# Attention in a macaron encoder layer: where the splits of the projection weights may run, and how the fourth part's projection steps are spread

## The chip, the cores and the metric

The kernel runs on one core of a Trainium2 chip. The metric is the device time in microseconds. The profile names five engines: PE (TensorE: matrix products and transposes; PEld is its weight load), DVE (VectorE), ACT (ScalarE), POOL (GpSimd) and SP (SyncE, which issues the DMAs).

## The reference

One layer: x = x + ½ SwiGLU(norm(x)), then x = x + attention(norm(x)), then x = x + ½ SwiGLU(norm(x)), for 1024 rows of 1024 in float32. The change lies in the attention, a stick-breaking one with 16 heads of 64:

```python
qkv = (xn @ w_qkv).reshape(b, s, 3, SB_HEADS, SB_HEAD_DIM)
q = rms_norm(qkv[:, :, 0], q_gain).astype(jnp.float32).transpose(0, 2, 1, 3)
k = rms_norm(qkv[:, :, 1], k_gain).astype(jnp.float32).transpose(0, 2, 1, 3)
v = qkv[:, :, 2].astype(jnp.float32).transpose(0, 2, 1, 3)
...
    z = jnp.einsum('bhqd,bhkd->bhqk', q[:, :, lo:hi], k[:, :, :hi]) * scale
...
    log_beta = jax.nn.log_sigmoid(z)
    log_1m = jnp.where(mask, jax.nn.log_sigmoid(-z), 0.0)
    rev = lax.cumsum(log_1m, axis=3, reverse=True)
...
    w = jnp.where(mask, jnp.exp(log_beta + rev_excl), 0.0)
    outs.append(jnp.einsum('bhqk,bhkd->bhqd', w, v[:, :, :hi]))
```

## The kernel before

Every product is made of three: an operand is split into a rounded high part (ScalarE copies it into the format that TensorE multiplies) and a low part (raw minus high), and TensorE computes high·high, high·low and low·high (lines 255 to 257). So weights must be split before they are used.

The attention works on heads in **pairs**, 0 to 7. Its plan is a list of (nominal time, step): `PAIR` is 61, cut into the parts a (10), b (14), c (21) and d (16). For every pair `put` and `spread` enter the steps at such times; sorted by them, they are traced. The time is only an order: the tile framework then gives each engine its queue, taking what was traced first where several instructions are ready, and bringing forward later ones whose inputs and buffers are there. Within an engine's queue the order is then fixed.

In the turn of pair p stand:

- **scores** (lines 750 to 785) of four units, head 0 or 1 and half 1 or 0 of the queries. TensorE multiplies (L770), ScalarE takes two sigmoids (L774), VectorE scans (L776), GpSimd sets the first column (L781) and multiplies (L783). The unit of part d belongs already to pair p+1.
- **values** (lines 787 to 842) of the unit scored one part before: TensorE transposes w (L805), ScalarE and VectorE split it into th and tl (L168, L169), TensorE multiplies by v (L823). A finished half goes out through SyncE (L837).
- the **projection of pair p+1**, `qkv`: 24 steps, that is two halves of the rows (half 1 first), four blocks of 128 rows in each, three *thirds* of the eight 128-deep slices of the weights in each block (slices 0 to 2, 3 to 5, 6 and 7). `FILLS` says how many of them lie in each part: 4, 6, 8, 6. After the last third of a block `finish` squares and copies (L692, L693, ScalarE), and after the fourth block of a half VectorE works out the norms (L180 to L184), then r (L704), and GpSimd doubles the keys (L708 for head 0, L711 for head 1). The fourth block of half 1 ends early in c; the third block of half 0 is the first three steps of d, its fourth the last three.
- **prep_q** and **prep_k**: TensorE transposes queries and keys (L728), ScalarE and VectorE split them (L732, L733). `prep_k(nxt, 0, 1)` stands at c 17.5, `prep_q(this, 0)` at a 5.0 and `prep_k(this, 0, 0)` at a 7.5; the last two read half 0, which ended in d of the turn before, and prep_k what L708 wrote.
- the **weights of pair p+2**, `weights_of`, in pairs 0 to 5: four steps of two slices each. A step loads 2 x 192 KB into one of two buffers `raw_qkv` (L657, two DMAs of SyncE), ScalarE makes the high part (L660) and GpSimd two low parts (L663). Slices 0 to 3 and 4 to 7 have a tile each for high and low; four such sets take turns (`wq0` to `wq3`), so those of pair p+2 are written where those of pair p stood. `LOADS` puts the steps at a 6.0, b 8.0, d 2.0 and d 8.0. They need nothing but their raw data and the set of tiles, which the projection of pair p frees at the end of the turn p-1.

The last turn in which weights are split is that of pair 5; the turn of pair 6 still projects pair 7, that of pair 7 projects nothing.

Of the kernel before, what the change touches and what calls it, by code (L numbers as in the profile page):

```python
# [13 lines left out]
ALU = mybir.AluOpType  # L14
# [28 lines left out]

FILLS = {"a": 4, "b": 6, "c": 8, "d": 6}

LOADS = (("a", 6.0), ("b", 8.0), ("d", 2.0), ("d", 8.0))

SHARES = (("b", 6.0), ("b", 11.0), ("c", 3.0), ("c", 9.0), ("c", 15.0), ("d", 1.5), ("d", 5.0), ("d", 8.5))

# [49 lines left out]
def macaron_kernel(ctx, tc, x, g1, w1_in, w1_out, gm, w_qkv, gq, gk, w_o, g2, w2_in, w2_out, out):  # L99
    nc = tc.nc  # L100
    act, dve, pool_e, pe, sp = nc.scalar, nc.vector, nc.gpsimd, nc.tensor, nc.sync
# [533 lines left out]
    with ExitStack() as stack:  # L635
# [6 lines left out]
            sp.dma_start(t, src)  # L642
            g_sb.append(t)

        def weights_of(p, state):

            wh, wl = state["wq"] = {}, {}

            def step(k):
                if k % 4 == 0:  # L650
                    wq = pl[f"wq{(2 * p + k // 4) % 4}"]
                    state["h"], state["l"] = (wq.tile([P, 4, 3 * P], F32R, name=f"wq{n}", bufs=1) for n in "hl")
                h_, l_ = state["h"], state["l"]
                raw = pl["raw_qkv"].tile([P, 2, 3, P], F32, name="raw_qkv")
                src = w_qkv[k * P : (k + 2) * P, :].rearrange("(k p) (a c) -> p k a c", p=P, a=3)
                for i in range(2):
                    sp.dma_start(raw[:, i], src[:, i, :, p * P : (p + 1) * P])  # L657
                ks = slice(k % 4, k % 4 + 2)
                raw = raw.rearrange("p k a c -> p k (a c)")
                act.activation(h_[:, ks], raw, AF.Copy)  # L660
                for i in range(2):
                    k_ = k % 4 + i
                    pool_e.tensor_tensor(l_[:, k_, :], raw[:, i, :], h_[:, k_, :].bitcast(F32), op=ALU.subtract)  # L663
                    wh[k + i], wl[k + i] = h_[:, k % 4 + i, :], l_[:, k % 4 + i, :]

            return [partial(step, k) for k in ((4, 6, 0, 2) if p == 0 else (0, 2, 4, 6))]

        def qkv(p, state):

# [181 lines left out]
        states = [{} for _ in range(NP)]  # L851
        plan = []

        def spread(steps, t0, t1, at=0.5):
            plan.extend((t0 + (t1 - t0) * (i + at) / len(steps), f) for i, f in enumerate(steps))

        steps = qkv(0, states[0])
        for f in weights_of(0, states[0]):
            f()
# [8 lines left out]
        dve.tensor_copy(first[:, :P], ident)  # L868
        spread(steps[12:], -26.0, -6.0)
        spread(weights_of(1, states[1]), -20.0, -2.0)  # L870
        for p in range(-1, NP):
            this = states[p] if p >= 0 else None
            nxt = states[p + 1] if p < NP - 1 else None
            start, t = {}, PAIR * p
            for part, span in PARTS.items():
                start[part], t = t, t + span

            def put(part, t, f):
                plan.append((start[part] + t, f))

            for part, span in PARTS.items():
                state = nxt if part == "d" else this
                if state is not None:
                    spread(scores(state, *UNITS[part]), start[part], start[part] + span, 0.5)
                if this is not None:
                    groups = values(this, p, *BEFORE[part])
                    for i, (to_turn, to_apply) in enumerate(groups):
                        t = TURN + (span - TURN) * i / len(groups)
                        put(part, t, to_turn)
                        put(part, t + APPLY, to_apply)  # L890
            if nxt is not None:
                if p >= 0:
                    fills = qkv(p + 1, nxt)
                    for part, span in PARTS.items():
                        for i in range(FILLS[part]):
                            put(part, span * (i + 0.5) / FILLS[part], fills.pop(0))
                put("c", 15.0, partial(prep_q, nxt, 1))
                put("c", 17.5, partial(prep_k, nxt, 0, 1))
                put("d", 8.0, partial(prep_k, nxt, 1, 1))
            if this is not None:  # L900
                put("a", 5.0, partial(prep_q, this, 0))
                put("a", 7.5, partial(prep_k, this, 0, 0))
                put("b", 8.0, partial(prep_k, this, 1, 0))
            if 0 <= p < NP - 2:
                for at, f in zip(LOADS, weights_of(p + 2, states[p + 2])):
                    put(*at, f)
            if p == NP - 2:
                put("c", 10.0, partial(load_o, 1))
                put("d", 15.5, lambda: marks.append(tc.cur_priority))
            if p == NP - 1:  # L910
                put("a", 2.5, partial(load_o, 0))
                for at in SHARES:
                    put(*at, lambda: marks.append(tc.cur_priority))
# [126 lines left out]
```

## Time and profile before

| | us |
|---|---|
| median of 3 runs | 1998.88 (1997.27 to 1999.94) |
| the profiled execution | 1997.53 |
| its span | 1995.8 |
| of it: first feed-forward and norm, 0 to 657 | 657.0, TensorE busy 632.7 |
| first projections, 657 to 743 | 86.0, TensorE busy 76.4 |
| pairs, 743 to 1230 | 487.0, TensorE busy 464.6 |
| output projection and second feed-forward | 765.8, TensorE busy 752.4 |

The stretches come from the table of windows. In lists in order of time a row has start, duration, engine, line and operation, what it writes and reads, how many were merged, and in brackets the idle time of the engine before it and what ended that. The list of waits has the waiter, the one that ended the wait, the sum in us, how often, and the longest. A window's row has the length, then busy time and count of PE, PEld, DVE, ACT and POOL, the share of its clock that TensorE was granted, the share of time of the DMA engines, and GB/s. Where a window is asked for one line alone, only that line's engine stands in it.

### The profile page before, as it was taken

The numbers are of one execution on the slowest core, as the hardware profiler recorded it, in microseconds if no ns is written. First come the engines' busy times: TensorE is split into PE (matmuls) and PEld (weight loads), VectorE is DVE, ScalarE is ACT, GpSimd is POOL, SyncE is SP. The second block draws the span as 40 slices with busy tenths as digits, with TensorE's granted clock in tenths as the row PEclk, the third lists the DMA queues.
The fourth block names the chain that finished last, engine by engine and source line by source line (L and its number), as shares of the span: only waits on it lengthen the run. The fifth ranks groups of instructions, "written<-read, shape, count | busy, mean of one in ns | idle before, by whom it ended". The sixth has DMA issues, their size and how long they took to land.

```text
span 1995.8 us, 27301 instructions
## 1 busy us (share of the span) xinstructions
PE 1926.1 (97%) x9656; PEld 1651.9 (83%) x9656; DVE 1252.9 (63%) x1793; ACT 988.1 (50%) x1802; POOL 1092.0 (55%) x921
## 2 busy tenths in 40 slices
PE   7899999999999999999999999999999999999999
PEld 6788888887888789888888997779888888888887
DVE  6945644645675957768777787566654554547644
ACT  6443343343334557777777777443444334344332
POOL 2666666755456634655555455113666666755454
PEclk9999999999999999999999999999999999999999
DMA  5132332337997410111011045222332323359884
GB/s 206 64 101 101 116 101 85 126 113 261 332 320 256 139 39 13 54 43 38 28 54 38 14 145 169 85 90 64 122 101 90 122 96 101 105 190 359 317 270 152
DMA packets 168505, 260.26 MB, mean 130 GB/s; under 512 B 11568, under 2 KB 81200, under 8 KB 168368
## 3 DMA queue, kind: packets, MB, share of 16 engines
q1 hardware_dynamic: 168368, 258.52, 38.1%
q8 instruction: 75, 1.23, 0.2%
q14 instruction: 62, 0.51, 0.1%
HBM read 198.18 MB, written 60.29 MB: 130 GB/s over the span
## 4 chain that ended last, share of the span: by engine, by line
PE 79%; DVE 9%; POOL 4%; ACT 4%; issue 2%; DMA 1%; SPq 0%; ACTq 0%; POOLq 0%; DVEq 0%
PE ka L255 6%; PE ka L256 6%; PE ka L257 6%; PE kc L257 4%; PE kc L256 4%; PE kc L255 4%; PE bq L256 4%; PE bq L255 4%; PE bq L257 4%; PE ma L255 4%; PE kb L255 4%; PE kb L257 3%; PE kb L256 3%; PE ma L257 3%; PE ma L256 3%; PE bo L823 3%
## 5 line engine op out<-in xcount | busy, mean ns | idle before, releaser
L169 POOL TENSOR_TENSOR u<-sf,u 128x512 fp32r<-128x512 f32 x160 | 226.6, 1418 | 161.2 <-ACT u L168 160.4
L169 POOL TENSOR_TENSOR rp<-raw,rp 128x1024 fp32r<-128x1024 f32 x84 | 208.7, 2487 | 185.1 <-ACT rp L168 172.9
L169 POOL TENSOR_TENSOR u<-raw,u 128x512 fp32r<-128x512 f32 x136 | 199.8, 1473 | 167.3 <-ACT u L168 167.2
L783 POOL TENSOR_TENSOR w<-w,om 128x512 f32<-128x512 f32 (+4 forms) x128 | 140.8, 1103 | 142.1 <-DVE om L776 115.4
L168 ACT ACTIVATE u<-sf 128x512 fp32r<-128x512 f32 x160 | 100.9, 631 | 217.7 <-PE kb L256 89.8
L363 DVE TENSOR_TENSOR h<-h 128x512 f32<-128x512 f32 x110 | 134.7, 1228 | 90.0 <-POOL h L464 89.3
L255 PE MATMUL bq<-wqh,xh 128*128 128x384 f32 x512 | 177.7, 347 | 2.8 <-DVE vst L697 2.8
L168 ACT ACTIVATE rp<-rh 128x1024 fp32r<-128x1024 f32 (+1 forms) x78 | 76.6, 984 | 207.0 <-issue 86.5
L257 PE MATMUL bq<-wqh,xl 128*128 128x384 f32 x512 | 174.4, 341 | 0.0
L256 PE MATMUL bq<-wql,xh 128*128 128x384 f32 x512 | 174.3, 341 | 0.0
L255 PE MATMUL ka<-xh,u 128*128 128x512 f32 (+1 forms) x448 | 163.2, 365 | 9.8 <-ACT s L413 7.6
L256 PE MATMUL ka<-xl,u 128*128 128x512 f32 (+1 forms) x448 | 163.0, 364 | 1.2 <-DVE xl L169 1.2
L257 PE MATMUL ka<-xh,u 128*128 128x512 f32 (+1 forms) x448 | 162.6, 363 | 0.0
L168 ACT ACTIVATE u<-raw 128x512 fp32r<-128x512 f32 x136 | 84.6, 631 | 148.4 <-PE ka L256 101.8
L485 DVE TENSOR_TENSOR raw<-raw 128x1024 f32<-128x1024 f32 (+1 forms) x60 | 85.2, 1421 | 108.7 <-DMA raw<-w_out 97.6
L255 PE MATMUL ma<-rp 128*128 128x512 f32 x352 | 137.9, 392 | 2.0 <-DVE h L417 2.0
L774 ACT ACTIVATE w<-bz,f 128x512 f32<-128x512 f32 (+1 forms) x192 | 112.2, 584 | 55.5 <-PE bz L770 54.3
L256 PE MATMUL ma<-rp 128*128 128x512 f32 x352 | 137.6, 391 | 0.0
L257 PE MATMUL ma<-rp 128*128 128x512 f32 x352 | 137.5, 390 | 0.0
L390 DVE TENSOR_TENSOR sf<-raw 128x512 f32<-128x512 f32 x80 | 79.1, 990 | 89.3 <-POOL u L169 89.3
L464 POOL TENSOR_TENSOR h<-h,g 128x512 f32<-128x512 f32 x80 | 112.1, 1401 | 29.0 <-DVE h L417 29.0
L169 DVE TENSOR_TENSOR tl<-bt,th 128x512 fp32r<-128x512 f32 (+1 forms) x160 | 105.0, 657 | 30.1 <-ACT th L168 28.3
(219 smaller groups left out, 5573.7 us busy)
## 6 DMA issues: line engine op xcount, KB each, us to landing
raw<-w_out SPq DMA_DIRECT2D x120, 512.0 KB, 5.4
raw<-w_in SPq DMA_DIRECT2D x88, 512.0 KB, 3.6
k<-h SPq DMA_DIRECT2D x154, 256.0 KB, 2.0
rh<-k SPq DMA_DIRECT2D x64, 512.0 KB, 5.6
raw_qkv<-w_qkv SPq DMA_DIRECT2D x64, 192.0 KB, 2.9
x_keep<-x SPq DMA_DIRECT2D x32, 256.0 KB, 3.1
x<-x_keep SPq DMA_DIRECT2D x32, 256.0 KB, 5.0
raw<-w_out SPq DMA_DIRECT2D x24, 256.0 KB, 4.6
```

The costliest lines, as they stand in the source:

```text
L168: act.activation(hi, raw, AF.Copy)
L169: (engine or dve).tensor_tensor(lo, raw, hi.bitcast(F32), op=ALU.subtract)
L255: pe.matmul(dst, ah, bh, start=start and i == 0, stop=False, skip_group_check=onto)
L256: pe.matmul(dst, ah, bl, start=False, stop=False, skip_group_check=onto)
L257: pe.matmul(dst, al, bh, start=False, stop=stop and i == n - 1, skip_group_check=onto)
L363: dve.tensor_tensor(src, hb[of[0]], hb[of[1]], op=getattr(ALU, of[2]))
L390: dve.tensor_tensor(f[n], x, y, op=op)
L464: pool_e.tensor_tensor(h, h, gs[k], op=ALU.mult)
L485: dve.tensor_tensor(w[0], w[0], w[1], op=getattr(ALU, W_OF[m][2]))
L774: act.activation(to, z, AF.Sigmoid, scale=state["f", half][:, sign, tb % 4, hd : hd + 1])
L783: pool_e.tensor_tensor(wt[:, c1 : c0 + n], wt[:, c1 : c0 + n], om[:, c1 - 1 : c0 + n - 1], op=ALU.mult)
L823: pe.matmul(ot[:, :n], vv, t[:, c : c + n], start=start, stop=stop)
```

## The change

Three edits. `LOADS` puts the four steps of the weights later, at c 14.0, c 15.0, d 9.0 and d 10.0. For pairs 2 to 7 each step gets a small operation of GpSimd ahead of its split: it multiplies one column of another tile by itself and writes the product into the first column of the step's high part, which the split then overwrites. That column is the doubled keys of half 1 of pair p+1 (what L708 writes) for the first two steps, and the queries of the third block of half 0 of pair p+1 (what L693 writes) for the other two. So the split comes after these; the load does not. And the projection steps of part d are spread over 13 instead of 16: they stand at 1.1, 3.3, 5.4, 7.6, 9.8 and 11.9 instead of 1.3, 4.0, 6.7, 9.3, 12.0 and 14.7.

```diff
-LOADS = (("a", 6.0), ("b", 8.0), ("d", 2.0), ("d", 8.0))
+LOADS = (("c", 14.0), ("c", 15.0), ("d", 9.0), ("d", 10.0))
...
-        def weights_of(p, state):
+        def weights_of(p, state, behind=None):
...
-            def step(k):
+            def step(n, k):
...
                     sp.dma_start(raw[:, i], src[:, i, :, p * P : (p + 1) * P])
                 ks = slice(k % 4, k % 4 + 2)
                 raw = raw.rearrange("p k a c -> p k (a c)")
+                if behind:
+                    there = behind[n]()
+                    pool_e.tensor_tensor(h_[:, k % 4, 0:1], there, there, op=ALU.mult)
                 act.activation(h_[:, ks], raw, AF.Copy)
...
-            return [partial(step, k) for k in ((4, 6, 0, 2) if p == 0 else (0, 2, 4, 6))]
+            return [partial(step, i // 2, k) for i, k in enumerate((4, 6, 0, 2) if p == 0 else (0, 2, 4, 6))]
...
-                            put(part, span * (i + 0.5) / FILLS[part], fills.pop(0))
+                            put(part, (span - (3.0 if part == "d" else 0.0)) * (i + 0.5) / FILLS[part], fills.pop(0))
...
-                for at, f in zip(LOADS, weights_of(p + 2, states[p + 2])):
+
+                held = (lambda s=nxt: s["qk", 1][:, 0, 4, 0:1], lambda s=nxt: s["qk", 0][:, 2, 0, 0:1])
+                for at, f in zip(LOADS, weights_of(p + 2, states[p + 2], held)):
                     put(*at, f)
```

## The prediction

> **What bounds the kernel now.** I read the page first, then the list of waits of TensorE, then the attention stage in stretches, then single engines in time order around the longest wait.
>
> ```profile
> span 1995.8 us, 27301 instructions
> PE 1926.1 (97%) x9656; PEld 1651.9 (83%) x9656; DVE 1252.9 (63%) x1793; ACT 988.1 (50%) x1802; POOL 1092.0 (55%) x921
> ...
> PE bz L728 <- POOL qk L708: 15.0, 5, 3.0
> PE bt L805 <- POOL w L781: 5.1, 8, 0.7
> ```
>
> TensorE is busy 97% of the span, so time can only come from its waits and from a slow clock. Its largest wait in attention is one sort: the transposes of the keys (L728, prep_k) wait five times, up to 3.0 us, for GpSimd's doubling of the keys (L708). These rows show one case (TensorE, GpSimd, VectorE):
>
> ```profile
> 877.09 0.40 PE L823 MATMUL bo<-tl,vst 128*128 128x512 f32 x1
> 880.49 1.11 PE L728 MATMUL bz<-ident,qk 128*128 128x128 f32 x4 [3.00 <-POOL qk L708]
> ...
> 875.50 1.99 POOL L663 TENSOR_TENSOR wql<-raw_qkv,wqh 128x384 fp32r<-128x384 f32 x2
> 877.50 0.98 POOL L783 TENSOR_TENSOR w<-w 128x383 f32<-128x383 f32 x1
> 878.45 0.98 POOL L663 TENSOR_TENSOR wql<-raw_qkv,wqh 128x384 fp32r<-128x384 f32 x1
> 879.40 1.04 POOL L708 TENSOR_TENSOR qk<-qk,r 128x512 f32<-128x512 f32 x1
> ...
> 875.87 0.17 DVE L704 TENSOR_SCALAR r<-bq 128x8 f32<-128x8 f32 x1
> ```
>
> The factor r that L708 needs is there at 875.87 + 0.17 = 876.04. L708 starts 3.36 us later, because three low parts of weights (L663: 1.99 + 0.98 = 2.97 us) and one L783 stand ahead of it on GpSimd. These L663 belong to the weights of the pair after next; nobody needs them for most of a pair.
>
> I then cut each pair at three transposes: prep_q of half 0 (plan: a 5.0), prep_k of head 0, half 0 (a 7.5), prep_k of head 0, half 1 (c 17.5). **Stretch Y** runs from the first to the second; its columns are length, busy time (count) of PE, PEld, DVE, ACT, POOL, granted clock, DMA share, GB/s. Of Y: pair 0, the first and last of the five pairs 1 to 5 (all 5.68 to 5.70), pair 6.
>
> ```profile
> 738.17:743.19 5.02, 3.23 (x18) 2.26 (x18) 2.24 (x9) 3.48 (x7) 5.02 (x6) 0.98 0.29 79
> 806.81:812.49 5.68, 2.68 (x20) 2.25 (x18) 5.21 (x13) 4.22 (x10) 5.68 (x8) 1.00 0.37 115
> ...
> 1085.08:1090.76 5.68, 2.69 (x20) 2.25 (x18) 5.21 (x13) 4.33 (x10) 5.68 (x8) 1.00 0.12 47
> 1154.41:1157.20 2.79, 2.68 (x19) 2.24 (x18) 2.62 (x10) 2.52 (x6) 2.74 (x4) 1.00 0.89 278
> ```
>
> Pair 6 is the control. It has the same projection, scores and values, but no weights left to split, and Y takes 2.79 instead of 5.68 us. **Stretch Z**, from there to c 17.5, pairs 0 to 6:
>
> ```profile
> 743.19:779.06 35.87, 35.22 (x202) 32.79 (x202) 28.77 (x56) 27.88 (x62) 21.10 (x31) 0.96 0.12 38
> 812.49:847.06 34.57, 33.74 (x200) 31.25 (x201) 26.28 (x50) 26.04 (x57) 20.45 (x30) 1.00 0.09 28
> 880.49:917.49 37.00, 36.37 (x200) 33.95 (x201) 26.42 (x50) 26.27 (x57) 20.21 (x30) 0.92 0.08 26
> 950.95:986.82 35.87, 35.26 (x200) 32.81 (x201) 26.41 (x50) 26.27 (x57) 20.21 (x30) 0.95 0.08 27
> 1020.25:1057.35 37.10, 36.49 (x201) 34.02 (x202) 26.43 (x50) 26.28 (x57) 20.22 (x30) 0.92 0.08 26
> 1090.76:1126.66 35.90, 35.27 (x201) 32.83 (x202) 26.43 (x50) 26.27 (x57) 20.21 (x30) 0.95 0.09 31
> 1157.20:1192.02 34.82, 33.96 (x200) 31.18 (x201) 28.59 (x55) 27.26 (x60) 19.35 (x29) 1.00 0.42 137
> ```
>
> With the clock at 1.00 Z takes 34.57 and 34.82; where it was granted less, 35.87 to 37.10. The low clock begins right behind the wait:
>
> ```profile
> 880.50:886.40 5.90, 5.90 (x23) 5.90 (x24) 1.87 (x3) 1.88 (x4) 3.37 (x7) 0.51 0.25 71
> 886.40:890.00 3.60, 3.60 (x23) 3.42 (x22) 1.54 (x2) 2.51 (x4) 0.10 (x1) 1.00 0.00 0
> ```
>
> So a wait costs its own length and, in four of the five, a stretch at half clock behind it.
>
> **The change part by part.** *Y loses the L663.* After the change the splits of pairs 2 to 7 may begin only when pair p+1's doubled keys of half 1 (steps 0 and 1) and its third block of half 0 (steps 2 and 3) exist, both in the second half of pair p, so they can no longer be taken in Y. What is late next: without L663, L783 (0.98) can follow the factor at 876.0 and L708 ends near 876.0 + 0.98 + 1.04 = 878.0, against TensorE free at 877.49: 0.5 us would be left. But the last three thirds of the projection are also traced earlier, the last at 13 x 5.5/6 = 11.9 instead of 14.7 of part d, 2.75 us, and the factor comes out of them; that covers the 0.5. So I take pair 6's length: 5 x (5.68 - 2.79) = 14.45 us. Pair 0: its wait is another one, with the same splits behind it:
>
> ```profile
> 740.56 0.84 ACT L660 ACTIVATE wqh<-raw_qkv 128x768 fp32r<-128x768 f32 x1 [0.96 <-DMA raw_qkv<-w_qkv]
> 741.94 0.50 PE L823 MATMUL bo<-th,vst 128*128 128x512 f32 x1 [1.56 <-ACT th L168]
> ```
>
> ScalarE waits for the load of weights that it splits, th stands behind it, TensorE waits for th. Gone with the splits: 5.02 - 2.79 = 2.23.
>
> *Z gets its clock back.* The mean of the two undisturbed lengths is 34.7; the five others sum to 181.74, less 5 x 34.7 = 173.5: 8.2 us.
>
> The Trainium skill speaks against this term: its page "TensorE: Matmul & The Clock Gate", section "HAM oscillation — how this bites in real kernels", puts the harm at idle gaps of TensorE over about 3.4 us, and none of these waits is longer than 3.0. Taken so, the low clock would have another cause and stay. The trace differs: 0.51 stands directly behind a wait of 3.00.
>
> *What comes into **stretch X*** (c 17.5 to the next a 5.0, parts c and d), where the splits now land. X of pair 3, with one lot of two splits (L660) and four L663 already in it, and of pair 5, which has none; then the L663 alone of the first:
>
> ```profile
> 986.82:1014.57 27.75, 27.61 (x172) 25.70 (x171) 20.81 (x39) 21.35 (x46) 12.18 (x19) 1.00 0.13 38
> 1126.66:1154.41 27.75, 27.61 (x173) 25.71 (x172) 20.87 (x38) 19.11 (x42) 8.37 (x15) 1.00 0.21 68
> ...
> 986.82:1014.57 27.75, 3.94 (x4) 1.00 0.13 38
> ```
>
> Same length with and without. One lot stays and one is added: ScalarE 21.35 + 2.2 = 23.6 and GpSimd 12.18 + 3.94 = 16.1 of 27.75 us. TensorE's 27.61 hides both, if the order holds. The holds are 24 operations of one column; no row has one, the nearest are these, so 0.10 to 0.46 us each, 0.4 to 1.8 us of GpSimd per pair:
>
> ```profile
> 970.04 0.10 POOL L781 MEMSET w<- 128x1 f32 x1
> 970.25 0.46 POOL L783 TENSOR_TENSOR w<-w,om 128x127 f32<-128x127 f32 x1
> ```
>
> Where they land in pair 3:
>
> ```profile
> 984.01 1.05 POOL L708 TENSOR_TENSOR qk<-qk,r 128x512 f32<-128x512 f32 x1
> 994.50 1.29 POOL L783 TENSOR_TENSOR w<-w,om 128x512 f32<-128x512 f32 x1 [4.13 <-DVE om L776]
> 1000.49 0.38 ACT L693 ACTIVATE qk<-bq 128x256 f32<-128x256 f32 x1
> 1004.87 0.10 POOL L781 MEMSET w<- 128x1 f32 x1 [3.04 <-ACT w L774]
> ...
> 1005.70 1.58 ACT L660 ACTIVATE wqh<-raw_qkv 128x768 fp32r<-128x768 f32 x2
> ...
> 1008.66 3.15 SPq L657 DMA_DIRECT2D raw_qkv<-w_qkv  x4
> 1012.81 0.33 SPq L837 DMA_DIRECT2D o_keeph<-w  x1
> ...
> raw_qkv<-w_qkv SPq DMA_DIRECT2D x64, 192.0 KB, 2.9
> ```
>
> The keys are doubled at 985.1 (first hold), the third block is copied at 1000.9 (second hold), and GpSimd idles 4.13 us up to 994.50 and 3.04 up to 1004.87: each gap takes most of a lot. Behind a waiting hold on GpSimd stand L783 (what TensorE transposes one part later) and the doublings. On SyncE, loads move too: those of steps 2 and 3 wait for buffers that the first lot frees near 994; with 3.15 for the four issues and 2.9 to land they are there at 1000, just as the hold opens. The output stores L837 come at 1012.81, behind all of that. The planner does bring ready work forward: the lot at 1005.70 is the one that the plan puts at a 6.0 and b 8.0 of pair 4, yet it runs before that pair's prep_q, a 5.0 (1014.57). The price of X lies between 0, the row with and without, and pair 0's accident in each of six pairs, a 1.56 wait and a low clock of 35.87 - 34.7 = 1.2: 6 x 2.7 = 16. Below nothing: the 0.7 us waits of L805 could shrink, at most 5.1. I take 0, since the nearest row is this very stretch. Fewer thirds at the end of d leave TensorE less to do between a transpose and its use; a part's first thirds can be brought forward into that, so 0 too, inside the same bounds.
>
> **Sum:** 14.45 + 2.23 + 8.2 = 24.9 us. The profiled execution took 1997.53 (span 1995.8 and 1.7 around it): 1972.6. The median of the runs is 1.35 higher: **1974**.
>
> **The rivals.** *A small wait in X takes the place of the one in Y*: ScalarE takes a split whose load is late, or GpSimd a lot ahead of an L783. For it: pair 0. Against: X with a lot in it shows none. 1974 + 16 = 1990. *Only the waits go, the clock stays*: 1974 + 8.2 = 1982. For it: 812.49, where a wait of 3.0 drew no low clock, so the tie is loose. This is what that rule of the Trainium skill would give. *The change does nothing*: the planner slides the second lot behind the fourth block again, because loads or buffers come late, and L663 stand before L708 as now: 1999. Against: 8 us between the copy of the third block and that of the fourth. *Slower*: the second hold is queued on GpSimd ahead of an L783 that is due, waits there for the third block, and a whole lot (3.94) follows. Scans, then TensorE, wait; say 3.94 and the longer low clock, 37.00 - 34.7 = 2.3, in each of six pairs: 37, so 1974 + 37 = 2011. It decides from 24.9 / 6 = 4.15 us per pair. Against it: GpSimd idles 15 us of X.
>
> **How the numbers follow.** Forecast 0.60, small waits 0.14, clock stays 0.06, nothing 0.08, slower 0.12. A measurement of this kernel can tell about 0.2%, 4 us. Faster: 0.60 + 0.14 + 0.06 = 0.80; same 0.08; slower 0.12. The range runs from 1969, the forecast less the 5.1 of L805, to 1994, past the small waits with their 16 and one measurement's width: 0.80 in it.
>
> **What would show it.** L728 for L708 gone from TensorE's waits; Y of pairs 1 to 5 near 2.8; Z at 34.6 to 34.8 with clock 1.00; no L663 in Y; X at 27.75 with eight L663 in it. An X of 30 us, or waits of TensorE for th or w there, would speak for the small waits or the slow case; Y at 5.7, for nothing.

## The result: half of the gain, and the profile after

| | us | ratio to before, 95% interval |
|---|---|---|
| before, median of 4 | 1999.16 (1997.27 to 1999.94) | |
| after, median of 4 | 1985.69 (1982.75 to 1987.26) | 0.9939 (0.992 to 0.9958) |
| after, profiled execution | 1986.43, span 1984.1 | |

The kernel is faster by 13.5 us; 24.9 were forecast. In the changed file the lines are six higher: the hold is L665, the split L666, the low parts L669, the doublings L714 and L717, the key transposes L734, the scan L782, GpSimd's product L789, the product with v L829 (all of TensorE, ScalarE, VectorE, GpSimd as before).

From the page and the list of TensorE's waits, after:

```profile
span 1984.1 us, 27296 instructions
PE 1922.3 (97%) x9656; PEld 1643.5 (83%) x9656; DVE 1261.7 (64%) x1793; ACT 985.8 (50%) x1802; POOL 1094.8 (55%) x945
...
PE bo L829 <- ACT th L168: 5.6, 9, 1.0
PE bt L811 <- POOL w L787: 4.3, 7, 0.6
PE bo L829 <- DVE tl L169: 3.4, 12, 0.7
...
PE bz L734 <- POOL qk L714: 0.6, 2, 0.4
```

The wait for the doubled keys went from 15.0 to 0.6 us. In its place TensorE now waits for th (1.6 before, 5.6 after) and tl (1.8 and 3.4). GpSimd's 24 more instructions are the holds.

One thing in the prediction's names must be put right before its stretches are used: the transposes at which it ends Z and begins X are those of `prep_q` at c 15.0, not those of `prep_k` at c 17.5, which come 3 us later. The lengths in its rows are not touched by that. Y, Z and X of pair 3 after the change (columns as in the prediction), and then the first piece of X, from c 15.0 to c 17.5, after and before (before with three rows of TensorE at its start and the two of ScalarE that matter there):

```profile
938.54:941.15 2.61, 2.61 (x19) 2.35 (x18) 2.58 (x7) 2.44 (x6) 1.82 (x3) 1.00 0.54 201
941.15:976.42 35.27, 34.25 (x201) 31.22 (x200) 27.75 (x52) 25.93 (x58) 19.68 (x31) 1.00 0.05 16
976.42:1005.38 28.96, 28.06 (x172) 25.74 (x171) 21.95 (x43) 22.99 (x52) 16.94 (x26) 1.00 0.19 55
...
976.42:980.89 4.47, 3.57 (x21) 2.91 (x20) 3.43 (x5) 4.47 (x12) 3.77 (x5) 1.00 0.11 29
```

```profile
986.82:989.89 3.07, 3.07 (x21) 2.90 (x20) 2.82 (x4) 2.29 (x5) 1.67 (x3) 1.00 0.00 0
...
986.82 0.60 PE L728 MATMUL bz<-ident,qk 128*128 128x128 f32 x4
987.18 0.48 PE L823 MATMUL bo<-th,vst 128*128 128x512 f32 x1
987.49 0.40 PE L823 MATMUL bo<-tl,vst 128*128 128x512 f32 x1
...
983.85 0.38 ACT L692 ACTIVATE sq<-bq 128x256 f32<-128x256 f32 x1
...
984.97 0.60 ACT L168 ACTIVATE th<-bt 128x512 fp32r<-128x512 f32 x1 [0.29 <-PE bt L805]
```

Y is at 2.61, the clock is 1.00 throughout, but X has grown by 1.2, from 27.75 to 28.96. One piece, with the same 21 products and transposes on TensorE, has grown by 1.4, and the rest of X is 0.2 shorter. The same piece of pair 2 in order of time, ScalarE, GpSimd and TensorE:

```profile
908.73 0.85 ACT L666 ACTIVATE wqh<-raw_qkv 128x768 fp32r<-128x768 f32 x1 [2.06 <-POOL wqh L665]
909.48 0.37 ACT L698 ACTIVATE sq<-bq 128x256 f32<-128x256 f32 x1
...
910.16 0.61 ACT L168 ACTIVATE th<-bt 128x512 fp32r<-128x512 f32 x1
...
906.74 1.06 POOL L714 TENSOR_TENSOR qk<-qk,r 128x512 f32<-128x512 f32 x1
907.88 0.62 POOL L717 TENSOR_TENSOR qk<-qk,r 128x256 f32<-128x256 f32 x1
908.44 0.10 POOL L787 MEMSET w<- 128x1 f32 x1
908.50 0.35 POOL L665 TENSOR_TENSOR wqh<-qk 128x1 fp32r<-128x1 f32 x2
...
909.57 0.60 PE L734 MATMUL bz<-ident,qk 128*128 128x128 f32 x4
910.82 0.49 PE L829 MATMUL bo<-th,vst 128*128 128x512 f32 x1 [0.66 <-ACT th L168]
911.55 0.50 PE L829 MATMUL bo<-tl,vst 128*128 128x512 f32 x1 [0.23 <-DVE tl L169]
```

ScalarE stands idle for 2.06 us in front of the first split, until GpSimd has written the hold at 908.50, behind both the doubling and one L717. The copies of a block (L698 and two more) and th are queued behind that split. Before the change no split stood there: th began at 984.97, in front of the transposes at 986.82. So TensorE reaches the product with th before th is there. From the transposes to the product with th it takes 910.82 - 909.57 = 1.25 us (0.36 in the rows of pair 3 before), and from there to the one with tl 0.73 (0.31): 0.89 + 0.42 = 1.3 of the 1.4.

All pairs in one row, from prep_q of pair 0 to prep_q of pair 7, before and after:

```profile
738.17:1217.31 479.14, 455.75 (x2700) 421.32 (x2700) 363.18 (x694) 358.36 (x777) 258.83 (x367) 0.98 0.17 53
```

```profile
738.19:1202.67 464.48, 450.71 (x2700) 411.80 (x2699) 363.31 (x694) 356.89 (x779) 264.80 (x395) 1.00 0.17 56
```

The pairs won 14.7 us. What lies behind them, up to the end of the span, went from 1995.8 - 1217.31 = 778.5 to 1984.1 - 1202.67 = 781.4 and gave 2.9 back; what lies ahead was equal. 14.7 - 2.9 = 11.8 against a span shorter by 11.7.

### The profile page after: what moved, and what is told of

Read it like the earlier page. It is cut to its first block, busy times and chain, and to the rows that moved or that the text cites. A ratio compares the mean times of both kernels' runs of the same rounds, so it can differ in the third digit from the quotient of the medians.

```text
span 1984.1 us, 27296 instructions
## 1 busy us (share of the span) xinstructions
PE 1922.3 (97%) x9656; PEld 1643.5 (83%) x9656; DVE 1261.7 (64%) x1793; ACT 985.8 (50%) x1802; POOL 1094.8 (55%) x945
## 4 chain that ended last, share of the span: by engine, by line
PE 81%; DVE 10%; ACT 3%; POOL 3%; issue 2%; DMA 1%; SPq 0%; ACTq 0%; POOLq 0%; DVEq 0%
PE ka L255 6%; PE ka L256 6%; PE ka L257 6%; PE kc L256 4%; PE kc L255 4%; PE kc L257 4%; PE bq L256 4%; PE bq L255 4%; PE kb L255 4%; PE bq L257 4%; PE kb L256 4%; PE kb L257 4%; PE ma L255 4%; PE ma L257 4%; PE ma L256 4%; PE bo L829 3%
## 5 line engine op out<-in xcount | busy, mean ns | idle before, releaser
L789 POOL TENSOR_TENSOR w<-w,om 128x512 f32<-128x512 f32 (+4 forms) x128 | 141.0, 1104 | 120.3 <-DVE om L782 93.9
L780 ACT ACTIVATE w<-bz,f 128x512 f32<-128x512 f32 (+2 forms) x192 | 112.9, 588 | 46.2 <-PE bz L776 43.0
L169 DVE TENSOR_TENSOR rp<-rh,rp 128x1024 fp32r<-128x1024 f32 (+1 forms) x70 | 109.2, 1577 | 21.2 <-ACT rp L168 18.6
```

The source lines that it names most:

```text
L169: (engine or dve).tensor_tensor(lo, raw, hi.bitcast(F32), op=ALU.subtract)
L780: act.activation(to, z, AF.Sigmoid, scale=state["f", half][:, sign, tb % 4, hd : hd + 1])
L789: pool_e.tensor_tensor(wt[:, c1 : c0 + n], wt[:, c1 : c0 + n], om[:, c1 - 1 : c0 + n - 1], op=ALU.mult)
```

## The experiments

The theories. **A**: ScalarE's queue stops at the first split, which waits for the hold, and th behind it is late. **B**: the thirds of part d, traced closer, leave TensorE too little between its products. A rival to both: the floor that the prediction took from pair 6 was never there.

**The floor: no loads and no splits at all.** Part d as before the change.

```diff
-                for at, f in zip(LOADS, weights_of(p + 2, states[p + 2], held)):
-                    put(*at, f)
+                states[p + 2]["wq"] = states[p]["wq"]
...
-                            put(part, (span - (3.0 if part == "d" else 0.0)) * (i + 0.5) / FILLS[part], fills.pop(0))
+                            put(part, span * (i + 0.5) / FILLS[part], fills.pop(0))
```

> Leaves out the loads and splits of the weights of pairs 2 to 7 (these pairs project with the weights of pairs 0 and 1), thirds of part d over 16: the floor that the prediction took from pair 6. By the prediction Y 2.79, Z 34.7 and X 27.75 in every pair, 1974 within 2 us. If Y, Z and X sum to 66.5 or more here too, the floor itself was wrong: pair 6 was not a control, and the 1.7 us per pair have nothing to do with where the splits run.

1972.91 us (ratio 0.9892, 0.9873 to 0.9911). Its windows: all pairs, Z of pair 3, X of pair 3:

```profile
738.79:1194.15 455.36, 446.87 (x2700) 411.04 (x2699) 362.13 (x692) 341.90 (x755) 217.45 (x323) 1.00 0.11 36
937.79:972.59 34.80, 33.93 (x201) 31.15 (x201) 28.59 (x55) 27.27 (x60) 19.35 (x29) 1.00 0.04 16
972.59:1000.33 27.74, 27.61 (x172) 25.71 (x171) 20.92 (x38) 19.13 (x42) 8.42 (x15) 1.00 0.03 10
```

With Y at 2.80 this is the floor as the prediction drew it: 479.14 - 24.9 = 454.2 was forecast for the pairs, 455.4 came. The rival falls; pair 6 was a fair control for a pair without splits. What it could not show is the price of the splits in their new place.

**The holds alone**, part d over 16:

```diff
-                            put(part, (span - (3.0 if part == "d" else 0.0)) * (i + 0.5) / FILLS[part], fills.pop(0))
+                            put(part, span * (i + 0.5) / FILLS[part], fills.pop(0))
```

> The later LOADS and the holds, with the thirds of part d over 16 as before. Theory A (the first hold: ScalarE's first split waits for GpSimd's hold behind L708, and th stands behind that split): the wait of TensorE for th in stretch X, 0.66 us in each of six pairs after the change, stays, and the time is that of the changed kernel, 1986 within 3. Theory B (the thirds traced closer leave TensorE too little between its products): X falls from 28.97 back to about 27.8 and Z from 35.3 to 34.7 per pair, so 6 x 1.8 = 11 us less, near 1975. If the 0.5 us that I left in Y without the closer thirds is real, 3 us are added to either.

1981.49 (0.9924, 0.9911 to 0.9938). The pairs take 464.9, as with both edits; the piece c 15.0 to c 17.5 stays at 4.43 to 4.49 in pairs 0 to 5, and Y is 2.86. So B does not explain the pairs. The median is 1.5 us below the 1983 to 1989 that theory A gave; the profiled execution is 4.4 shorter than that of the changed kernel, 2.5 of it ahead of the pairs and 2.3 behind them, with pairs 0.4 longer. The 0.5 us that the closer thirds were to cover in Y did not come: 2.86 against 2.80 without any split.

**The closer thirds alone**:

```diff
-LOADS = (("c", 14.0), ("c", 15.0), ("d", 9.0), ("d", 10.0))
+LOADS = (("a", 6.0), ("b", 8.0), ("d", 2.0), ("d", 8.0))
...
-                for at, f in zip(LOADS, weights_of(p + 2, states[p + 2], held)):
+                for at, f in zip(LOADS, weights_of(p + 2, states[p + 2])):
```

> The thirds of part d over 13, with LOADS as before and no holds. The splits are free to run in Y again. Theory A: the waits for L708 come back but shorter by up to the 2.75 us by which the last third is earlier, since the L663 stand in the way all the same: Y between 3 and 5.7, no wait for th in X, time between 1976 and 1999, and X as before at 27.8. Theory B: X 28.5 or more without any hold. If Y is 2.8 here, the holds were not needed at all.

1996.73, no change (1.0005, 0.9996 to 1.0014). Y and Z of pair 3, and the longest of TensorE's waits in the list over all pairs:

```profile
942.58:947.15 4.57, 2.97 (x20) 2.28 (x18) 4.37 (x11) 3.65 (x8) 4.51 (x5) 1.00 0.30 86
947.15:984.42 37.27, 35.73 (x201) 32.74 (x201) 28.21 (x55) 27.52 (x62) 20.39 (x30) 0.95 0.12 40
...
PE bo L829 <- ACT th L168: 6.0, 6, 2.2
```

Y falls only to 4.5 to 4.8 in pairs 1 to 5, the clock is low again behind it, and X is 27.3. So the closer thirds alone are not enough, the splits have to leave Y; in X they do no harm. No run has the later `LOADS` without any hold, so what the later place does by itself is not shown.

**The first hold later**:

```diff
-LOADS = (("c", 14.0), ("c", 15.0), ("d", 9.0), ("d", 10.0))
+LOADS = (("c", 20.0), ("c", 20.5), ("d", 9.0), ("d", 10.0))
...
-                held = (lambda s=nxt: s["qk", 1][:, 0, 4, 0:1], lambda s=nxt: s["qk", 0][:, 2, 0, 0:1])
+                held = (lambda s=nxt: s["qk", 0][:, 1, 0, 0:1], lambda s=nxt: s["qk", 0][:, 2, 0, 0:1])
```

> The changed kernel with the first hold moved: it reads the queries of the second block of half 0 of the next pair (written by ScalarE some 8 us after the doubled keys), and its two steps are put at c 20.0 and c 20.5. Theory A: the wait for th in X goes (0.66 and the 0.23 for tl behind it), and with 0.9 to 1.3 us per pair the time is 5 to 8 us below the changed kernel, 1978 to 1981. Theory B: X keeps its 28.9 apart from that wait, and the time is within 3 us of 1986.

1975.66 (0.9893, 0.9877 to 0.9909), 10 below the changed kernel and lower than either theory had it. All pairs, and the piece c 15.0 to c 17.5 of pair 2:

```profile
733.19:1190.34 457.15, 447.94 (x2701) 410.81 (x2700) 361.09 (x694) 359.77 (x779) 264.43 (x395) 1.00 0.18 57
902.82:905.87 3.05, 3.05 (x22) 2.88 (x21) 2.82 (x4) 2.27 (x5) 1.67 (x3) 1.00 0.00 0
```

7.3 us of the pairs' 9.1 above the floor are gone, as theory A has it. (The two profiled executions differ by 13.7: these 7.3, another 5.0 ahead of the pairs, where no edit reaches, and 1.4 behind them.) But this edit moves the hold and the split together. Is it the wait, or the split's own 0.85 us in front of th?

**The same split, its hold on another engine**:

```diff
-                    pool_e.tensor_tensor(h_[:, k % 4, 0:1], there, there, op=ALU.mult)
+                    (pool_e if n else dve).tensor_tensor(h_[:, k % 4, 0:1], there, there, op=ALU.mult)
...
-                r = pl["sq"].tile([P, 4, 4], F32, name="r", bufs=1)
+                r = state["r", half] = pl["sq"].tile([P, 4, 4], F32, name="r", bufs=1)
...
-                held = (lambda s=nxt: s["qk", 1][:, 0, 4, 0:1], lambda s=nxt: s["qk", 0][:, 2, 0, 0:1])
+                held = (lambda s=nxt: s["r", 1][:, 0, 0:1], lambda s=nxt: s["qk", 0][:, 2, 0, 0:1])
```

> The changed kernel with the first hold on VectorE instead of GpSimd: it reads r of half 1, which VectorE writes itself one step before GpSimd doubles the keys. The order of ScalarE's instructions around the first split stays that of the changed kernel. Theory A1 (the loss is ScalarE waiting, 2.06 us, for GpSimd's hold, with the copies and th queued behind): the split starts as soon as ScalarE is free, TensorE's wait for th goes, and the piece from prep_q c 15.0 to prep_k c 17.5 falls from 4.46 to about 3.06 us; 6 x 1.4 = 8.4 us off the pairs. Theory A2 (the loss is the split's own 0.85 us ahead of th, wherever the hold is): the piece stays above 3.7 and the time within 4 us of the changed kernel.

1979.81 (0.9921, 0.9909 to 0.9934). ScalarE in pair 2, the piece, and TensorE just before it:

```profile
904.82 0.84 ACT L666 ACTIVATE wqh<-raw_qkv 128x768 fp32r<-128x768 f32 x1 [0.17 <-DVE wqh L665]
...
906.54 0.60 ACT L168 ACTIVATE th<-bt 128x512 fp32r<-128x512 f32 x1 [0.16 <-PE bt L811]
...
908.32:911.35 3.03, 3.03 (x21) 2.86 (x20) 2.90 (x4) 2.90 (x6) 3.03 (x4) 1.00 0.02 5
...
905.51 0.50 PE L829 MATMUL bo<-tl,vst 128*128 128x512 f32 x1 [0.73 <-DVE tl L169]
```

The split stands where it stood in ScalarE's order, still 0.84 us long, but waits 0.17 instead of 2.06, and the piece is back at 3.03. It was the wait and not the split: A1 holds. VectorE charges for its part: two holds, 0.91 us together, stand in its queue in front of a tl, and TensorE waits 0.73 for that tl one piece earlier (c 15.0 comes 24.1 instead of 23.3 us after prep_k of head 1, b 8.0). The pairs take 459.5: 5.0 of the 8.4 us stay won.

**The later hold, with part d over 16**:

```diff
-                            put(part, (span - (3.0 if part == "d" else 0.0)) * (i + 0.5) / FILLS[part], fills.pop(0))
+                            put(part, span * (i + 0.5) / FILLS[part], fills.pop(0))
```

> The first hold on the second block's queries as in the run before, and the thirds of part d over 16 as before the change. If the closer thirds cost nothing per pair and some 2 us behind the pairs (the last pair's prep_q to the end took 781.4, 780.1 and 781.0 us with them, 778.5 to 779.2 without), this is the fastest: pairs 0 to 6 near 456 us, where the run with the closer thirds took 457 and the one without splits 455, and 1972 to 1975 in all. If the closer thirds are needed once the splits are in X, Y rises above 3.3 and it is slower than the run with them.

1975.06 (0.9906, 0.9891 to 0.9921): as good as with the closer thirds, not to be told from it. The pairs take 458.6 (forecast near 456), the rest 1972.7 - 1194.04 = 778.7.

**The changed kernel once more**, no edit:

> The changed kernel once more, beside the others on this chip: 1986 within 3, the pairs 0 to 6 at 464.5 us and the piece c 15.0 to c 17.5 at 4.46, as every theory has it.

1983.89 (0.9944, 0.9932 to 0.9957), pairs 464.5, piece 4.47 to 4.48: as expected.

**No splits, closer thirds**: the first edit above without its second part.

> Leaves out the loads and splits of pairs 2 to 7 (they project with the weights of pairs 0 and 1), with the thirds over 13: what the closer thirds cost by themselves, against the run without splits at 1973. By the run with the closer thirds alone, nothing in the pairs (65.2 us each, 65.4 without them) and 2 us from the last pair on: 1974 to 1976. If the closer thirds did the harm, the pairs would be 66 or longer.

1975.36 (0.9894, 0.9878 to 0.991). The pairs take 453.7, 1.7 less than with part d over 16; behind them 1968.3 - 1188.16 = 780.1 against 779.1. In all kernels with the closer thirds that rest is 780.1 to 782.1, in all with 16 it is 778.5 to 779.3. So the closer thirds cost some 2 us there, and save 0.4 to 1.7 in the pairs: 464.5 against 464.9 with both holds, 457.1 against 458.6 with the first hold later, 453.7 against 455.4 without splits.

**One hold each.** First only the second one:

```diff
-LOADS = (("c", 14.0), ("c", 15.0), ("d", 9.0), ("d", 10.0))
+LOADS = (("a", 6.0), ("b", 8.0), ("d", 9.0), ("d", 10.0))
...
-                if behind:
+                if behind and n == 1:
```

(and part d over 16)

> Of the two holds only the second one stays (first two steps free, at a 6.0 and b 8.0 as before; thirds over 16). By theory A1 all the harm is in the first hold, and the good is done by keeping splits out of Y. In this program's order both lots stand on GpSimd ahead of the doubling of half 0's keys, in part d, one behind the other. So: c 15.0 to c 17.5 at 3.06, Y at 2.9, pairs 0 to 6 at 455 to 459 us, 1973 to 1977 in all. If eight L663 in part d are too many there, Y goes above 3.5 and the time above 1980.

1991.84 (0.9978, 0.9969 to 0.9987), well above the 1973 to 1977 that I expected; the pairs take 474.0. ScalarE and TensorE late in pair 1 and early in pair 2:

```profile
863.29 0.84 ACT L666 ACTIVATE wqh<-raw_qkv 128x768 fp32r<-128x768 f32 x1 [3.04 <-DMA raw_qkv<-w_qkv]
...
866.90 0.38 PE L829 MATMUL bo<-th,vst 128*128 128x256 f32 x1 [1.30 <-ACT th L168]
...
876.33 0.66 PE L734 MATMUL bz<-ident,qk 128*128 128x128 f32 x4 [1.24 <-POOL qk L714]
```

The piece is at 3.06, as forecast, but now splits stand in ScalarE's queue ahead of their data: 3.04 us for a load, th behind it again, the norms and the doubling late too (Y 3.8 to 4.5 in pairs 1 to 5; above 3.5 was the expectation's other case). Then only the first hold:

```diff
-LOADS = (("c", 14.0), ("c", 15.0), ("d", 9.0), ("d", 10.0))
+LOADS = (("c", 14.0), ("c", 15.0), ("d", 2.0), ("d", 8.0))
...
-                if behind:
+                if behind and n == 0:
```

(and part d over 16)

> Of the two holds only the first one stays (last two steps free, at d 2.0 and d 8.0; thirds over 16). The first hold keeps both lots out of Y, since the second lot's loads wait for the buffers of the first. By theory A1 the piece from c 15.0 to c 17.5 stays at 4.46 and ScalarE waits some 2 us for the hold; pairs 0 to 6 near 465 us as with both holds, 1980 to 1985. If that piece falls to 3.1 here, the wait needs both holds, and A1 is wrong as I put it.

2002.20 (1.0027, 1.0013 to 1.0042): slower than before, by 0.3%, where I expected 1980 to 1985. The pairs take 483.0. Pair 2:

```profile
911.10 0.85 ACT L666 ACTIVATE wqh<-raw_qkv 128x768 fp32r<-128x768 f32 x1 [2.06 <-POOL wqh L665]
...
918.15 0.85 ACT L666 ACTIVATE wqh<-raw_qkv 128x768 fp32r<-128x768 f32 x1 [1.74 <-DMA raw_qkv<-w_qkv]
...
920.96 0.39 PE L829 MATMUL bo<-th,vst 128*128 128x256 f32 x1 [1.55 <-ACT th L168]
```

Y is at 2.86 and the piece at 4.46, both as expected, but a second cost stands behind them. The free second lot follows at once, and its split waits 1.74 us for its load: 13.0 to 14.9 us from c 17.5 to d 8.0, where the floor has 10.6. My expectation had let the loads out. ScalarE's idle time in front of the splits, for loads alone, sums to 2.6 us before the change, to 18.1 with the second hold alone and to 9.9 with the first alone; in the changed kernel there is none. So there no split is queued before its data; with the first hold later some are again (6.4 us). Both of these kernels with one hold change a place in `LOADS` together with a hold, so the share of each is open. More buffers for the raw weights would be the direct test of the late loads; no run has them.

## Why the prediction was half right

- *The wait in Y, 14.45 + 2.23 = 16.7*: right. Pairs 1 to 5 gave 5 x (5.68 - 2.61) = 15.4 and pair 0 5.02 - 3.09 = 1.9.
- *The clock in Z, 8.2*: the mechanism was right: in the pairs no stretch at low clock is left. Those five Z sum to 175.7 instead of 181.7, so 6.1; Z itself is 35.3 with the closer thirds and 34.8 without. In pairs 1 and 6, which had nothing to win, it grew by 0.7 and 1.7. In pair 6 of the changed kernel the profile also shows ScalarE idle for 1.55 us up to 1144.42 until an output store (o_keeph) has landed; th is late behind it, and TensorE waits 0.96 for it.
- *The Trainium skill's rule* (page "TensorE: Matmul & The Clock Gate", section "HAM oscillation — how this bites in real kernels", idle gaps over about 3.4 us): by it the low clock would have stayed, and the time would have been 1982. The measurement decides against it. The low clock went with the waits, and came back with the closer thirds alone (0.95 in Z of pair 3 above), where TensorE's longest single wait in the pairs is 2.2 us.
- *"I take 0" for X*: **the step that failed.** X costs 28.96 - 27.75 = 1.2 us per pair, 7.4 in six, inside the bounds 0 to 16 but not at the end that I chose. Against the floors with the same thirds it is more: 28.96 - 27.3 = 1.7 with part d over 13, 29.3 - 27.75 = 1.5 with part d over 16. Of the 13.1 us between the forecast 24.9 and the 11.8 that came, X is 7.4, the smaller gain in Z 4.5 and the stretch behind the pairs 2.9; Y and pair 6 give 1.7 back. The row that I took it from shows a lot that the planner was free to place, with nothing to wait for. The change puts a held one there. Had I followed the hold through ScalarE's queue, as I did on GpSimd's, the rival of small waits, "ScalarE takes a split", would have been the likeliest case: it names the right engine, though the cause was the hold and not a late load.
- *The closer thirds at 0*: right within a microsecond or two in the pairs, but 2.9 us were lost behind them, about 2 of it by the closer thirds in every kernel that has them. Why the last pair and the output projection are longer with them was not settled; the low clock there is part of it in two of the five kernels (6.8 us at half speed in the changed one and 10.2 with the hold on VectorE, where all the others have 3.4).
- *L708 delayed by 0.5 without the closer thirds*: did not happen (2.86 against 2.80).

The sum by what was measured: 17.3 in Y, 6.1 - 0.7 - 1.7 = 3.7 in Z, -7.4 in X, +1.1 in pair 6 outside Z, 14.7 in the pairs, -2.9 behind them.

## What to carry to other kernels

A dependence that only orders work costs little by itself (two holds took GpSimd 0.35 us), but in ScalarE's queue everything behind the held instruction was held too: follow the queue of the engine that waits, not only that of the engine that writes the hold, and let the hold read something that is written well before the held instruction's turn comes. A free instruction that costs nothing in a stretch is no proof that a held one will not. And check a chosen place for each input: where one lot of splits was left free, splits stood in front of late loads, and the kernel with the first hold alone was slower than the one with none.

## What was not expected of the hardware

- Stretches at half clock are 3.4 or 6.8 us long in the pairs of these traces, and they need no single long wait: five came in the kernel with the closer thirds alone, with waits of at most 2.2 us; yet one wait of 3.0 us before the change drew none. The clock records say more. Before the change the low stretches of the pairs begin at 742.98, 879.51, 951.19, 1019.46 and 1091.14, which are 40, 21, 20 and 21 steps of 3.413 us apart. If all time is cut into such steps, the wait that drew none, up to 812.49, falls on two of them, with 1.76 and 1.24 us of idle TensorE; the other four put 2.0 to 3.0 into one step. With the closer thirds alone, the five steps just ahead of low stretches have 1.6 to 2.2 us of idle time in all. In the pairs of the twelve profiled executions a low stretch began behind every step with 1.6 us or more of idle time but that one of 1.76, and behind none with 1.5 or less. So in these traces the low clock goes with the idle time summed over one step, not with the length of a single wait.
- The work ahead of pair 0, which no edit touches, ended anywhere from 733.2 to 738.8 us after the start in the twelve profiled executions. Differences of 2 to 4 us between medians here are therefore read from the pairs, not from the total.
- A one-column operation took GpSimd 0.19 to 0.20 us (two in 0.35), nearer to the 0.10 of the MEMSET than to the 0.46 of the product of 127 columns.
